# A float32 decoder layer in split products on one core: the point in the gated MLP from which products run side by side, moved by one unit

## The chip, the cores and the metric

The kernel runs on one core of a Trainium2 chip. The metric is the device time of one execution in microseconds (us). Three runs of the kernel before are given and their median is used; the profile is of one further execution, whose own time is shown beside its span.

## What is computed

The program is one decoder layer for 256 rows of 1024 channels: a norm, a combined projection, three attention mixers, gates, an output projection and a residual. Then comes the part that the change touches, a gated MLP with a causal convolution of width 3, and a last norm:

```python
def conv_ffn(x, w_up, conv_w, conv_b, w_down):
    h = x @ w_up
    h = lax.conv_general_dilated(h, conv_w[:, None, :].astype(h.dtype), window_strides=(1,),
                                 padding=[(CONV_WIDTH - 1, 0)],
                                 dimension_numbers=('NWC', 'WIO', 'NWC'),
                                 feature_group_count=h.shape[-1]) + conv_b
    a, u = jnp.split(h, 2, axis=-1)
    return (jax.nn.silu(a) * u) @ w_down
...
        x = x + conv_ffn(rmsnorm(x, norm_ffn[i]), w_up[i], conv_w[i], conv_b[i], w_down[i])
```

`w_up` is 1024 by 5632 (gate half and up half), `w_down` is 2816 by 1024.

## The kernel before

Every float32 operand of a large product is held as two fp32r parts, a high part (the value rounded) and a low part (the rest), and a product a·b is the sum of three: low·high, high·low and high·high. Weights arrive in tiles of 1 MB (class `Unit`, line 205): SyncE loads `raw` (line 217), ScalarE writes the high part `whi` in two halves (line 222), VectorE the low part `wlo` in two halves (line 226). There are five buffers for `raw` and five for each part, used in turn.

The MLP goes through 11 units (line 971, `i` from 0 to 10). A unit takes 256 channels of the gate half (tile `fa`), the same 256 of the up half (`fu`) and 256 rows of `w_down` (`fd`), and works on two chunks of 128 channels (line 977). A chunk has an up product with `fa` and one with `fu` (function `up`, line 980), a convolution of each on ScalarE and VectorE (lines 965 and 967, tile `cy`), silu and the gate product (lines 1001 and 1003, tile `sa`), the split of the result into `fh` and `fl` (lines 1006 and 1007) and, one chunk later, the 12 down products that add to four sums `acc` (line 1008, `later`, line 760).

An up product sums over 8 slices of 128 input channels (k) and gives 128 channels by 256 rows. It is written in two ways:

- In the units below `NORMED` (lines 983 to 986) it takes the activations without the factor of the norm. For each k, `mm3` (line 237) issues three matmuls of 256 columns, on lines 238, 239 and 240, with `h_hi` and `h_lo` (tile `hn`). The result is multiplied by the norm's factor row by row when VectorE takes it out of PSUM (`by_rstd`, line 864).
- From unit `NORMED` on (lines 987 to 998) it takes the normed activations from `h_parts` (tile `parts`), where high and low part lie beside each other. For each k one matmul of 512 columns (line 988) multiplies the high weights with both, and one of 256 columns (line 990) the low weights with the high activations. ScalarE copies one half of the PSUM bank (line 996), VectorE adds the other (line 997).

Unit 0 is computed before the loop (lines 883 to 951). `h_parts` is made by `norm_parts(i)` (line 874), called for two halves of the channels (line 976): VectorE multiplies `whole` (tile `gl`) by the norm's factor (line 876), ScalarE writes the high part (line 877), VectorE the low part (line 878), each on 128 by 1024 elements. It is called in unit `NORMED - 1`, after that unit's weight tiles have been asked for (lines 973 to 976).

An up product's result needs one of four PSUM banks (`bank`, line 742), which is free when line 864 (or 996 and 997) has read it. On an engine, instructions run in the order in which the scheduler has put them at compile time; in the MLP's loop that order is the scheduler's, not the program's, for VectorE, ScalarE and TensorE alike. An instruction that waits holds up all that stand behind it on its engine.

Of the kernel before, what the change touches and what calls it, by code (L numbers as in the profile page):

```python
# [15 lines left out]

P = 128
WARM = 9
NORMED = 3
S = 256  # L20
D = 1024
KC = D // P
# [107 lines left out]
def decoder_layer(ctx: ExitStack, tc, x, small_b, table, w1, wts, norms, out):  # L130
# [103 lines left out]
    def unit(name, steps=2, eng=None):  # L234
        return Unit(name).split(steps, eng)
# [506 lines left out]
    def bank():  # L742
        turn[0] ^= 1
        return pools[turn[0]].tile([P, 512], F32, name="g")
# [226 lines left out]
    for i in range(NFF // 2):  # L971
        with tc.issue_after(on_act[3 + i].ins) if i in (1, 2) else ExitStack():
            ua, uu, ud = [fu.pop(f"f{w}{i}", None) or unit(f"f{w}{i}") for w in "aud"]
        if i == NORMED - 1:
            for part in range(2):
                norm_parts(part)
        for c in range(2):
            ch = 2 * i + c

            def up(u):  # L980
                cols = slice(c * P, (c + 1) * P)
                ps = bank()
                if i < NORMED:
                    for k in range(KC):
# [102 lines left out]
```

## Time and profile before

| what | value |
|---|---|
| median of 3 runs | 424.89 us (424.8 to 426.27) |
| the profiled execution's own time | 424.76 us |
| its span | 423.0 us |
| TensorE, VectorE, ScalarE busy, share of the span | 98%, 74%, 61% |
| mean granted clock of TensorE | 0.996 |

The times are of whole executions; the profile covers the span from its first to its last instruction, 1.76 us less than that execution's time. A view by order of time gives the start and the duration of each instruction; consecutive instructions of an engine overlap a little, so what one adds to a full queue is the distance from its start to the start of the next, not its duration.

### The profile page before, as it was taken

Reading aid. Unit: us, or ns where it says so; the run is one execution under the profiler, and the core shown is the slowest. Engines: PE = TensorE matmul, PEld = TensorE weight load, DVE = VectorE, ACT = ScalarE, POOL = GpSimd, SP = SyncE. Lnnn points to the kernel's source line nnn. Section 1 sums busy time; section 2 is a strip of 40 time slices with the busy share of each in tenths; the row PEclk is TensorE's granted clock in tenths of the full one; section 3 lists DMA queues with packets and bytes.
Section 4 is the critical chain, followed back from the end, with each engine's and each line's share of the span. In section 5 each row is a group of like instructions: output and inputs, shape, how many; then the busy total and the mean of one; then the engine's idle time right before and its main releaser. Section 6 shows DMA issues by size and latency. Waiting matters only on the chain.

```text
span 423.0 us, 6337 instructions
## 1 busy us (share of the span) xinstructions
PE 412.4 (98%) x2407; PEld 347.8 (82%) x2407; DVE 313.2 (74%) x624; ACT 256.2 (61%) x451; POOL 18.3 (4%) x28
## 2 busy tenths in 40 slices
PE   8999999999999999999999999999999999999993
PEld 7998778776667888878788998988888888888883
DVE  3996653788784888434753899998797797887765
ACT  5843283547787855555434889467476576584633
POOL 2500010120000000000000000000000000000001
PEclk9999999999999999999999999999999999999998
DMA  8999419532227793645350465565652743800002
GB/s 279 416 375 407 146 34 354 198 131 100 101 100 248 292 381 109 229 184 198 107 192 0 149 253 198 200 251 200 245 212 105 283 187 110 299 0 2 0 2 99
DMA packets 12750, 78.00 MB, mean 184 GB/s; under 512 B 1408, under 2 KB 1424, under 8 KB 4912
## 3 DMA queue, kind: packets, MB, share of 16 engines
q1 hardware_dynamic: 12144, 75.48, 47.8%
q0 software_dynamic: 576, 2.12, 1.4%
q8 instruction: 19, 0.31, 0.3%
q14 instruction: 11, 0.09, 0.1%
HBM read 76.52 MB, written 1.07 MB: 183 GB/s over the span
## 4 chain that ended last, share of the span: by engine, by line
PE 82%; DVE 8%; ACT 5%; DMA 2%; issue 2%; SPq 0%; POOLq 0%; POOL 0%; ACTq 0%
PE g L988 12%; PE g L239 10%; PE g L240 10%; PE g L238 10%; PE g L990 6%; PE acc L238 6%; PE acc L240 6%; PE acc L239 6%; PE g L298 3%; DVE wlo L226 2%; PE g L888 2%; PE o L541 2%; DMA raw<-in_wts_dram 2%; PE g L426 2%; PE g L300 1%
## 5 line engine op out<-in xcount | busy, mean ns | idle before, releaser
L226 DVE TENSOR_TENSOR wlo<-raw,whi 128x1024 fp32r<-128x1024 f32 (+2 forms) x131 | 154.1, 1201 | 41.0 <-ACT whi L222 40.6
L222 ACT ACTIVATE whi<-raw 128x1024 fp32r<-128x1024 f32 (+2 forms) x130 | 130.2, 1040 | 50.5 <-PE g L240 34.3
L988 PE MATMUL g<-parts,whi 128*128 128x512 f32 x256 | 89.4, 396 | 0.0
L990 PE MATMUL g<-parts,wlo 128*128 128x256 f32 x256 | 66.2, 279 | 0.0
L988 PEld LDWEIGHTS g<-parts,whi 128*128 128x128 f32 x256 | 46.7, 188 | 9.2
L990 PEld LDWEIGHTS g<-parts,wlo 128*128 128x128 f32 x256 | 48.2, 188 | 2.8
L239 PE MATMUL g<-wlo,hn 128*128 128x512 f32 (+1 forms) x128 | 50.0, 391 | 0.0
L240 PE MATMUL g<-whi,hn 128*128 128x512 f32 (+1 forms) x128 | 50.0, 391 | 0.0
L238 PE MATMUL g<-whi,hn 128*128 128x512 f32 (+1 forms) x128 | 49.8, 390 | 0.0
L967 DVE SCALAR_TENSOR_TENSOR cy<-xn,small_b,cy 128x255 f32<-128x255 f32 (+1 forms) x88 | 41.5, 480 | 9.0 <-ACT cy L965 8.0
L238 PE MATMUL acc<-whi,fl 128*128 128x512 f32 (+1 forms) x88 | 34.2, 389 | 0.1
L239 PE MATMUL acc<-wlo,fh 128*128 128x512 f32 (+1 forms) x88 | 34.0, 386 | 0.0
L240 PE MATMUL acc<-whi,fh 128*128 128x512 f32 (+1 forms) x88 | 34.0, 386 | 0.0
L965 ACT ACTIVATE cy<-xn,small_b 128x256 f32<-128x256 f32 x44 | 25.8, 598 | 7.4 <-DVE xn L997 7.4
L239 PEld LDWEIGHTS g<-wlo,hn 128*128 128x128 f32 x128 | 24.1, 188 | 5.1 <-issue 0.9
L240 PEld LDWEIGHTS g<-whi,hn 128*128 128x128 f32 x128 | 24.1, 188 | 4.2 <-issue 0.2
L238 PEld LDWEIGHTS g<-whi,hn 128*128 128x128 f32 x128 | 24.1, 189 | 4.0 <-ACT whi L222 0.2
L426 PE MATMUL g<-hn,whi 128*128 128x512 f32 x72 | 26.2, 405 | 0.0
L996 ACT ACTIVATE xn<-g 128x256 f32<-128x256 f32 x32 | 12.2, 380 | 22.2 <-PE g L988 22.2
L428 PE MATMUL g<-hn,wlo 128*128 128x256 f32 x72 | 19.9, 292 | 0.0
L997 DVE TENSOR_TENSOR xn<-g,xn 128x256 f32<-128x256 f32 x32 | 13.5, 421 | 8.3 <-ACT xn L996 8.3
L240 PEld LDWEIGHTS acc<-whi,fh 128*128 128x128 f32 x88 | 16.5, 188 | 3.4
(213 smaller groups left out, 698.6 us busy)
## 6 DMA issues: line engine op xcount, KB each, us to landing
raw<-in_wts_dram SPq DMA_DIRECT2D x61, 1024.0 KB, 4.8
gl<-in_w_dram SPq DMA_DIRECT2D x8, 512.0 KB, 7.6
raw<-in_wts_dram SPq DMA_DIRECT2D x5, 512.0 KB, 7.4
raw<-in_wts_dram SPq DMA_DIRECT2D x2, 804.0 KB, 9.0
T<-tvd POOLq DMA_DIRECT2D x1, 1280.0 KB, 16.3
xs<-in_x_dram SPq DMA_DIRECT2D x2, 516.0 KB, 3.8
out_dram<-raw SPq DMA_DIRECT2D x4, 256.0 KB, 2.1
T<-tvd POOLq DMA_DIRECT2D x1, 768.0 KB, 9.6
```

The costliest lines, as they stand in the source:

```text
L222: nc.scalar.activation(self.parts[0][:, sl], self.raw[:, sl], AF.Copy)
L226: return (eng or nc.vector).tensor_sub(self.parts[1][:, sl], self.raw[:, sl], self.parts[0][:, sl].bitcast(F32))
L238: nc.tensor.matmul(ps, al, bh, start=start, stop=False)
L239: nc.tensor.matmul(ps, ah, bl, start=False, stop=False)
L240: nc.tensor.matmul(ps, ah, bh, start=False, stop=stop)
L426: hi = lambda: nc.tensor.matmul(ps, view(0, k), h_parts[:, k].rearrange("p a q -> p (a q)"), start=k == 0, stop=k == KC - 1)
L428: lo = lambda: nc.tensor.matmul(ps[:, :S], view(1, k), h_hi[:, k, :], start=False, stop=False)
L965: on_act.append(nc.scalar.activation(y, u, AF.Identity, bias=vec_c[:, 3, ch:ch + 1], scale=vec_c[:, 2, ch:ch + 1]))
L967: nc.vector.scalar_tensor_tensor(y[:, sh:], u[:, :S - sh], vec_c[:, w, ch:ch + 1], y[:, sh:], op0=ALU.mult, op1=ALU.add)
L988: hi = lambda: nc.tensor.matmul(ps, u[0][:, k, cols], h_parts[:, k].rearrange("p a q -> p (a q)"), start=k == 0, stop=k == KC - 1)
L990: lo = lambda: nc.tensor.matmul(ps[:, :S], u[1][:, k, cols], h_parts[:, k, 0, :], start=False, stop=False)
L997: nc.vector.tensor_add(v, ps[:, :S], part)
```

## The change

One constant is smaller by one:

```diff
-NORMED = 3
+NORMED = 2
```

So `norm_parts` is called in unit 1, after unit 1's weight tiles and before its products (line 974), and unit 2 takes the second form of the up product (line 983). The four up products of unit 2 are then 32 matmuls of 512 columns and 32 of 256 in place of 96 of 256, and their results leave PSUM through lines 996 and 997 in place of line 864. The scheduler orders the loop anew.

On VectorE, the place is in unit 1 and the start of unit 2. In the names, `sa_2531` and `fl_2539` belong to chunk 0, `fl_2555` to chunk 1, `wlo_2572` to `fd` of unit 1, `g_2578` to `g_2689` (before) and `g_2584` to `g_2695` (after) are unit 1's four up products, and `wlo_2738` (before) and `wlo_2744` (after) are the low part of unit 2's `fa`. Before, from chunk 1's convolution to the first half of unit 2's `fa`:

```order
L967 SCALAR_TENSOR_TENSOR cy_2549<-xn1_2267,small_b_389,cy_2549 128x255
L226 TENSOR_TENSOR wlo_2572<-raw_2570,whi_2571 128x1024
L967 SCALAR_TENSOR_TENSOR cy_2549<-xn1_2267,small_b_389,cy_2549 128x254
L226 TENSOR_TENSOR wlo_2572<-raw_2570,whi_2571 128x1024
L1003 TENSOR_TENSOR sa_2546<-sa_2546,cy_2549 128x256
L967 SCALAR_TENSOR_TENSOR cy_2604<-xn1_2267,small_b_389,cy_2604 128x255
L967 SCALAR_TENSOR_TENSOR cy_2636<-xn1_2267,small_b_389,cy_2636 128x255
L1007 TENSOR_TENSOR fl_2555<-sa_2546,fh_2554 128x256
L967 SCALAR_TENSOR_TENSOR cy_2604<-xn1_2267,small_b_389,cy_2604 128x254
L967 SCALAR_TENSOR_TENSOR cy_2636<-xn1_2267,small_b_389,cy_2636 128x254
L864 TENSOR_TENSOR xn1_2267<-g_2657,xn1_2267 128x256
L226 TENSOR_TENSOR wlo_2738<-raw_2736,whi_2737 128x1024
```

And now, first the stretch that begins with the two multiplications of line 876:

```order
L876 TENSOR_TENSOR gl_2269<-gl_2269,xn1_2267 128x1024
L1003 TENSOR_TENSOR sa_2531<-sa_2531,cy_2533 128x256
L967 SCALAR_TENSOR_TENSOR cy_2549<-xn1_2267,small_b_389,cy_2549 128x255
L876 TENSOR_TENSOR gl_2270<-gl_2270,xn1_2267 128x1024
L1007 TENSOR_TENSOR fl_2539<-sa_2531,fh_2538 128x256
L967 SCALAR_TENSOR_TENSOR cy_2549<-xn1_2267,small_b_389,cy_2549 128x254
L226 TENSOR_TENSOR wlo_2572<-raw_2570,whi_2571 128x1024
L1003 TENSOR_TENSOR sa_2546<-sa_2546,cy_2549 128x256
L226 TENSOR_TENSOR wlo_2572<-raw_2570,whi_2571 128x1024
L1007 TENSOR_TENSOR fl_2555<-sa_2546,fh_2554 128x256
L878 TENSOR_TENSOR parts_2268<-gl_2269,parts_2268 128x4x256
L878 TENSOR_TENSOR parts_2268<-gl_2270,parts_2268 128x4x256
```

and the rows that follow it directly, down to the first half of unit 2's `fa`:

```order
L864 TENSOR_TENSOR xn1_2267<-g_2584,xn1_2267 128x256
L864 TENSOR_TENSOR xn1_2267<-g_2616,xn1_2267 128x256
L864 TENSOR_TENSOR xn1_2267<-g_2663,xn1_2267 128x256
L967 SCALAR_TENSOR_TENSOR cy_2610<-xn1_2267,small_b_389,cy_2610 128x255
L967 SCALAR_TENSOR_TENSOR cy_2642<-xn1_2267,small_b_389,cy_2642 128x255
L967 SCALAR_TENSOR_TENSOR cy_2610<-xn1_2267,small_b_389,cy_2610 128x254
L967 SCALAR_TENSOR_TENSOR cy_2642<-xn1_2267,small_b_389,cy_2642 128x254
L967 SCALAR_TENSOR_TENSOR cy_2689<-xn1_2267,small_b_389,cy_2689 128x255
L864 TENSOR_TENSOR xn1_2267<-g_2695,xn1_2267 128x256
L1003 TENSOR_TENSOR sa_2614<-sa_2614,cy_2642 128x256
L967 SCALAR_TENSOR_TENSOR cy_2689<-xn1_2267,small_b_389,cy_2689 128x254
L226 TENSOR_TENSOR wlo_2744<-raw_2742,whi_2743 128x1024
```

Before, one row of line 876 stood ahead of the first half of unit 2's `fa`, and both rows of line 878 and the other of line 876 far behind it; now all four stand ahead of it, and three rows of line 864, which free PSUM banks and feed ScalarE's convolutions, have come behind them.

On TensorE, the place is where unit 2's up products begin (`g_2766` in both programs, and after also `g_2831`, the product of the same weights for the second chunk; `whi_2737` and `wlo_2738` before, `whi_2743` and `wlo_2744` after are the two parts of unit 2's `fa`, `fl_2642` and `fl_2648` chunk 2's result). Before, after the last row of unit 1's fourth up product `g_2689`:

```order
L240 MATMUL g_2689<-hn_2265,whi_2462 128x256
L238 MATMUL g_2766<-hn_2265,wlo_2738 128x256
L239 MATMUL g_2766<-hn_2265,whi_2737 128x256
L240 MATMUL g_2766<-hn_2265,whi_2737 128x256
L238 MATMUL g_2766<-hn_2265,wlo_2738 128x256
L238 MATMUL acc00_2523<-whi_2571,fl_2642 128x512
```

and now, after the last two rows of that product (`g_2695`):

```order
L239 MATMUL g_2695<-hn_2265,whi_2462 128x256
L240 MATMUL g_2695<-hn_2265,whi_2462 128x256
L988 MATMUL g_2766<-parts_2268,whi_2743 128x512
L988 MATMUL g_2831<-parts_2268,whi_2743 128x512
L990 MATMUL g_2766<-parts_2268,wlo_2744 128x256 x2
L988 MATMUL g_2766<-parts_2268,whi_2743 128x512
L238 MATMUL acc00_2523<-whi_2571,fl_2648 128x512
```

In both, the low part of unit 2's `fa` is first read at the boundary between unit 1's and unit 2's up products, and the down products of chunk 2 stand behind. Now the two matmuls ahead of it read the normed activations and the high part. On SyncE and GpSimd the rows are the same as before.

## Rows read from the trace of the kernel before

**Rows 1.** The page, engines' busy time, and the chain that ended last, by engine
```profile
PE 412.4 (98%) x2407; PEld 347.8 (82%) x2407; DVE 313.2 (74%) x624; ACT 256.2 (61%) x451; POOL 18.3 (4%) x28
...
PE 82%; DVE 8%; ACT 5%; DMA 2%; issue 2%; SPq 0%; POOLq 0%; POOL 0%; ACTq 0%
```

**Rows 2.** Waits of TensorE over the whole span (us in total, times, longest): the first
```profile
PE g L325 <- DVE whi L308: 1.3, 2, 0.9
```

**Rows 3.** Busy time by stretch: PE, PEld, DVE, ACT, POOL, then clock, DMA, GB/s
```profile
251.65:277.34 25.69, 25.69 (x172) 23.70 (x171) 25.59 (x41) 20.03 (x29) 0.00 (x0) 1.00 0.48 170
...
300.00:400.00 100.00, 100.00 (x535) 85.87 (x535) 80.91 (x135) 64.22 (x110) 0.00 (x0) 1.00 0.38 141
```

**Rows 4.** Order of time on TensorE (start us, us, what)
```profile
243.25 0.28 PE L238 MATMUL g<-hn,wlo 128*128 128x256 f32 x1
...
251.65 0.47 PE L238 MATMUL acc<-whi,fl 128*128 128x512 f32 x1
251.95 0.40 PE L239 MATMUL acc<-wlo,fh 128*128 128x512 f32 x1
...
256.28 0.40 PE L238 MATMUL acc<-whi,fl 128*128 128x512 f32 x1
...
259.03 0.28 PE L239 MATMUL g<-hn,whi 128*128 128x256 f32 x1
...
260.34 0.28 PE L238 MATMUL g<-hn,wlo 128*128 128x256 f32 x1
...
280.90 0.40 PE L988 MATMUL g<-parts,whi 128*128 128x512 f32 x1
...
283.72 0.40 PE L988 MATMUL g<-parts,whi 128*128 128x512 f32 x1
```

**Rows 5.** Order of time on VectorE (start us, us, what)
```profile
248.88 0.42 DVE L864 TENSOR_TENSOR xn<-g,xn 128x256 f32<-128x256 f32 x1
...
249.61 0.42 DVE L864 TENSOR_TENSOR xn<-g,xn 128x256 f32<-128x256 f32 x1
249.95 1.22 DVE L876 TENSOR_TENSOR gl<-gl,xn 128x1024 f32<-128x1024 f32 x1
251.08 0.42 DVE L1007 TENSOR_TENSOR fl<-sa,fh 128x256 fp32r<-128x256 f32 x1
251.41 0.48 DVE L967 SCALAR_TENSOR_TENSOR cy<-xn,small_b,cy 128x255 f32<-128x255 f32 x1
251.81 1.22 DVE L226 TENSOR_TENSOR wlo<-raw,whi 128x1024 fp32r<-128x1024 f32 x1
252.94 0.48 DVE L967 SCALAR_TENSOR_TENSOR cy<-xn,small_b,cy 128x254 f32<-128x254 f32 x1
...
257.06 1.21 DVE L226 TENSOR_TENSOR wlo<-raw,whi 128x1024 fp32r<-128x1024 f32 x1
...
267.31 1.22 DVE L878 TENSOR_TENSOR parts<-gl,parts 128x1024 fp32r<-128x1024 f32 x1
```

**Rows 6.** Order of time on ScalarE (start us, us, what)
```profile
255.34 1.99 ACT L222 ACTIVATE whi<-raw 128x1024 fp32r<-128x1024 f32 x2
257.24 0.40 ACT L1001 ACTIVATE sa<-cy 128x256 f32<-128x256 f32 x1
257.55 0.59 ACT L965 ACTIVATE cy<-xn,small_b 128x256 f32<-128x256 f32 x1
258.04 1.04 ACT L877 ACTIVATE parts<-gl 128x1024 fp32r<-128x1024 f32 x1
```

**Rows 7.** The page, groups by line: busy us, mean ns, idle before
```profile
L988 PEld LDWEIGHTS g<-parts,whi 128*128 128x128 f32 x256 | 46.7, 188 | 9.2
...
L996 ACT ACTIVATE xn<-g 128x256 f32<-128x256 f32 x32 | 12.2, 380 | 22.2 <-PE g L988 22.2
```

**Rows 8.** Busy time by stretch as in rows 3, at the end of the program
```profile
416.00:418.00 2.00, 0.53 (x5) 0.32 (x3) 1.50 (x5) 1.55 (x6) 0.15 (x1) 1.00 0.35 131
418.00:423.00 5.00, 0.00 (x0) 0.00 (x0) 0.75 (x1) 0.72 (x1) 0.40 (x1) 0.64 0.42 157
```

## The prediction

> **What bounds the kernel now.** I read the page first: TensorE is busy for 98% of the span and carries 82% of the chain that ended last; VectorE, with 74%, is second [rows 1]. The view of TensorE's waits lists five pairs, the longest in total 1.3 us, and all five belong to the parts ahead of the MLP [rows 2]. By stretches, TensorE has no gap from 251.65 to 277.34 us nor from 300 to 400 us, at a granted clock of 1.00 (2.4 GHz) [rows 3]. So in the MLP the time is the sum of what TensorE issues, and a change can gain only by taking work from TensorE and lose only by making it wait; what it loses isn't paid back, since there is no later gap to swallow it. The second thing to see in [rows 3] is that VectorE is busy for 25.59 of the 25.69 us in the very stretch into which the change moves VectorE's work, but for 81 of the later 100 us.
>
> **What TensorE saves.** The views by order of time give the distances from start to start. Between 243.25 and 251.65 stand 70 matmuls of 256 columns (counted in the program's order), 0.120 us each, so a k in the old form costs 0.360 us. Twelve down products take 259.03 - 256.28 = 2.75 us, 0.229 us per matmul of 512 columns. Eight k in the new form take 283.72 - 280.90 = 2.82 us, 0.3525 us for each [rows 4]. Unit 2 has 4 up products of 8 k: 32 x 0.0075 = **0.24 us saved**. It is small because both forms stream 768 columns for a k; only one matmul in three goes away.
>
> A rule of the Trainium skill promises more. The row: a weight load lasts 188 ns [rows 7], but a load and its matmul of 256 columns together advance TensorE by 0.120 us [rows 4], so the loads lie under the matmuls. The rule ("TensorE: Matmul & The Clock Gate", The mechanism, in the part on packing small matmuls): a weight load overlaps with running matmuls only where the two use different row groups of the array, so here it would not; and a load of 128 columns takes 107 ns (LDWEIGHTS, same page). By it 32 fewer loads would save an estimated 3.4 us, and the sum would be 0.8 us faster after the wait found below. The trace disagrees: 0.120 us leaves no room for that beside 256 columns.
>
> **What moves on VectorE.** The number of rows stays: line 997 replaces line 864 four times, at the same size. ScalarE gets four more copies of line 996, 0.38 us each [rows 7], 1.5 us on an engine that is idle for 5.7 us of [rows 3]'s first stretch; I cost them at nothing, and if that cover is gone they lengthen the wait for ScalarE, not TensorE's work. SyncE's and GpSimd's rows are the same; the weights' buffers are released some us later where the low parts are made later, and the trace has no wait of the MLP for a landing, so I take nothing there either.
>
> What costs is the order. Up to 248.88 VectorE's rows are the same. From there, 23 rows stand ahead of the first low half of unit 2's `fa` in the changed program (the second and third VectorE excerpts). Six of them work on 128 by 1024 elements (two each of lines 876, 226 and 878): 252.94 - 251.81 = 1.13 us each, and 251.08 - 249.95 = 1.13 for line 876; line 878, of the same size, as these. Eight are of line 967: 251.81 - 251.41 = 0.40. Nine are small (three of line 1003, two of 1007, four of 864): 249.95 - 249.61 = 0.34 and 251.41 - 251.08 = 0.33 [rows 5]. Sum: 6 x 1.13 + 8 x 0.40 + 9 x 0.335 = 6.78 + 3.20 + 3.02 = 13.0 us. So the low half begins at 261.88 and, with 1.21 us for itself, ends at 263.09.
>
> To this come two short gaps. The convolutions of unit 1 can start on ScalarE only when line 864 has read its bank, 0.42 us [rows 5], and last 0.59 us, 0.49 from one to the next [rows 6]. VectorE reaches its first line 967 about 1.0 us after the first of the three rows of line 864, when the first convolution's 0.42 + 0.59 is just over, and the second one 0.40 later, when the second's +0.49 is just over: 0.1 us in all. **The low half is ready at about 263.2 us**; before, it began at 257.06 [rows 5].
>
> **When TensorE wants it.** Before, TensorE reached its first matmul with that low half at 260.34 [rows 4], 2 us after it was ready, so the slack was there. The changed program has the same work up to that point (unit 1's four up products, the down products of chunks 0 and 1), then two matmuls of 512 columns: 260.34 + 2 x 0.23 = 260.80. The high half that these two read must come from ScalarE: behind three convolutions whose first starts when line 864 lets it. By VectorE's sum line 864 begins at 257.80 (248.88 + 8.92: the first twelve rows), so the three run from 258.3 to 259.8 at 0.49 each, and the high half takes 1.04 us, to 260.8. That delays the two matmuls by some 0.5 us, inside the wait that follows.
>
> How long TensorE takes from a release to full pace is shown once: `fl` of chunk 0 ended at 251.08 + 0.42 = 251.50 [rows 5]; the down products' second matmul started at 251.95, where 251.65 + 0.23 was due [rows 4], so pace was resumed as from 251.72, 0.22 us after the release. So the first matmul with the low half starts at 263.2 + 0.2 = 263.4 instead of 260.8: **a wait of 2.6 us**. The down products of chunk 2 behind it need the very next row of VectorE, 0.34 us later, and TensorE is then busy with the four matmuls ahead of them for 0.6 us: no further wait. The other low halves come every 1 to 2 us from there, while unit 2's up products take 2.8 us each: I count no second wait.
>
> **Sum.** + 2.6 - 0.24 = + 2.4 us. Against the profiled execution: span 423.0 + 2.4 = 425.4, time 424.76 + 2.4 = 427.2; against the median of the runs, which lies 0.13 us higher, 424.89 + 2.4 = **427.3 us**, 0.56% slower. Its bounds: without gaps and without the 0.22 us the wait is 263.09 - 260.80 = 2.3 us, 426.9; with gaps of 0.5 us on VectorE and the saving not realised it is 3.0 us, 427.9.
>
> **Rivals.**
> - *The cover holds.* TensorE reaches the low half after it is ready, as before, where the slack was 2 us; it decides at the first matmul of line 990, if VectorE finishes that half before 260.8. Then only the saving is left: 424.89 - 0.24 = 424.65, not slower. For it: no MLP wait exists now [rows 2]. Against it: VectorE would have to do 13.0 us of rows in 10.5, and has no gap to close in that stretch [rows 3]. Chance 0.10.
> - *The clock falls in the wait.* After its last matmul the granted clock stays 1.00 in the stretch to 418 us, in which TensorE is busy for 0.53 of 2 us, and is 0.64 on average in the 5 us without any matmul [rows 8]. At 1.2 GHz all of those 5 us would read 0.50, so 0.72 of them, 3.6 us, were at the lower level. If the 2.6 us wait brought as long a stretch at half pace, it would cost 1.8 us more: 429.1. Against it: the stretch with 1.5 us of idleness didn't lower it. Chance 0.05.
> - *A second wait.* Unit 2's `fu` or `fd` low halves, which stand behind the same queue, are late by one row of 1.13 us: 428.4. Chance 0.03.
> - *Loads count.* Each of the 32 loads taken away gives back its 188 ns: 6.0 us, 427.3 + 0.24 - 6.0 = 421.5. [rows 4] speaks against it. Beside it stands the skill's rule above. Chance 0.02.
> - That the change doesn't do what it says is excluded by the order: the new form stands there for unit 2.
>
> **Numbers.** The forecast has the remaining chance, 0.80. A measurement of this kernel can tell about 0.5%, 2.1 us, from no change, so "slower" begins at 427.0. The forecast's bounds, 426.9 to 427.9, lie mostly above: I put 0.61 of its 0.80 there and 0.19 below. Slower: 0.61 + 0.05 + 0.03, taken as 0.68; within 0.5%: 0.19 + 0.10, taken as 0.30; faster: 0.02. The range takes in the forecast's bounds, widened by 0.5 to 0.7 us because the runs shown differ by 1.5 us and the durations are rounded, and the second wait: 426.2 to 428.4; it leaves out the cover that holds, the clock and the loads, 0.17.
>
> **What would show it.** Right: TensorE's waits list line 990 (or its load) behind line 226 with some 2.6 us, near 261 to 263.4 us, preceded by some 0.5 us of line 988 behind ScalarE's line 222; VectorE is without a gap from 249 to 263; the new form appears 32 k times more, at 0.3525 us; the last 100 us look as before, moved by 2.4 us. Wrong: no gap in TensorE there (then the cover held and the sum of VectorE's rows was too high), a granted clock under 1.00 after the gap, a wait of unit 2's later products, or k in the new form that take less than 0.35 us.

## The result, and the profile after

| what | before | after |
|---|---|---|
| median of the compared runs | 424.85 us (6 runs, 424.58 to 426.27) | 428.42 us (6 runs, 427.22 to 428.66) |
| the profiled execution's own time | 424.76 us | 427.22 us |
| its span | 423.0 us | 425.2 us |

The ratio is 1.0071, with a 95% interval of 1.0053 to 1.009: slower by 0.7% (the quotient of the two medians is 1.0084). Forecast were 427.3 us and a range of 426.2 to 428.4, so the sign was right; the median lies at the range's upper end, 0.02 us above it, and 1.1 us over the forecast. The profiled execution (427.22) is the lowest of the six. It shows the forecast's mechanism almost to the tenth of a microsecond; what lies between it and the other five is a second effect, which took the experiments to find.

The page of after, engines' busy time, the chain by engine, and the groups of lines 988 and 990, which answer to [rows 1, 7]:

```profile
PE 412.2 (97%) x2375; PEld 345.4 (81%) x2375; DVE 313.8 (74%) x624; ACT 257.1 (60%) x455; POOL 18.3 (4%) x28
...
PE 77%; DVE 12%; ACT 5%; issue 2%; DMA 2%; SPq 0%; POOLq 0%; POOL 0%; ACTq 0%; DVEq 0%
...
L988 PE MATMUL g<-parts,whi 128*128 128x512 f32 x288 | 100.8, 396 | 0.4 <-ACT whi L222 0.4
L990 PE MATMUL g<-parts,wlo 128*128 128x256 f32 x288 | 74.5, 279 | 1.7 <-DVE wlo L226 1.7
```

TensorE has 32 matmuls fewer, and two idle times that did not exist: 0.4 us ahead of line 988 and 1.7 us ahead of line 990. VectorE's share of the chain went from 8% to 12%. Where it happens, in order of time on TensorE (start us, us, what, and in brackets the idle time before it and its releaser):

```profile
260.85 0.73 PE L988 MATMUL g<-parts,whi 128*128 128x512 f32 x2 [0.36 <-ACT whi L222]
263.31 0.50 PE L990 MATMUL g<-parts,wlo 128*128 128x256 f32 x2 [1.73 <-DVE wlo L226]
263.65 0.40 PE L988 MATMUL g<-parts,whi 128*128 128x512 f32 x1
263.88 0.39 PE L238 MATMUL acc<-whi,fl 128*128 128x512 f32 x1
...
266.61 0.28 PE L990 MATMUL g<-parts,wlo 128*128 128x256 f32 x1
...
267.67 0.28 PE L990 MATMUL g<-parts,wlo 128*128 128x256 f32 x1
```

Before, the first matmul with the low half started at 260.34 [rows 4]; now at 263.31, behind two of line 988 that take 0.46. That is 2.5 us later than the same queue without a wait (260.80). The two matmuls of line 990 behind the release take 0.34 us instead of 0.24 (263.31 to 263.65), so what follows is 2.6 us late. Down products follow at 263.88 without a gap. What TensorE waited for, in order of time on VectorE:

```profile
248.80 1.22 DVE L876 TENSOR_TENSOR gl<-gl,xn 128x1024 f32<-128x1024 f32 x1
...
250.67 1.22 DVE L876 TENSOR_TENSOR gl<-gl,xn 128x1024 f32<-128x1024 f32 x1
...
255.47 2.36 DVE L878 TENSOR_TENSOR parts<-gl,parts 128x1024 fp32r<-128x1024 f32 x2
257.75 1.08 DVE L864 TENSOR_TENSOR xn<-g,xn 128x256 f32<-128x256 f32 x3
258.90 2.16 DVE L967 SCALAR_TENSOR_TENSOR cy<-xn,small_b,cy 128x255 f32<-128x255 f32 x5
260.97 0.42 DVE L864 TENSOR_TENSOR xn<-g,xn 128x256 f32<-128x256 f32 x1
261.31 0.42 DVE L1003 TENSOR_TENSOR sa<-sa,cy 128x256 f32<-128x256 f32 x1
261.64 0.48 DVE L967 SCALAR_TENSOR_TENSOR cy<-xn,small_b,cy 128x254 f32<-128x254 f32 x1
262.03 1.22 DVE L226 TENSOR_TENSOR wlo<-raw,whi 128x1024 fp32r<-128x1024 f32 x1
```

and on ScalarE, the high half that line 988 waited for:

```profile
258.26 1.59 ACT L965 ACTIVATE cy<-xn,small_b 128x256 f32<-128x256 f32 x3 [3.72 <-DVE xn L864]
259.76 1.04 ACT L222 ACTIVATE whi<-raw 128x1024 fp32r<-128x1024 f32 x1
```

By stretch (columns as in [rows 3]), the loss is in one place, and the rest is full as before:

```profile
260.50:263.80 3.30, 1.22 (x5) 0.79 (x6) 3.30 (x8) 3.30 (x7) 0.00 (x0) 1.00 0.00 0
263.80:277.00 13.20, 13.20 (x70) 11.23 (x69) 12.96 (x19) 9.52 (x14) 0.00 (x0) 1.00 0.73 263
300.00:400.00 100.00, 100.00 (x534) 85.79 (x533) 81.18 (x135) 63.14 (x108) 0.00 (x0) 1.00 0.39 144
```

### The profile page after: what moved, and what is told of

It reads as the page before. It is cut to its first block, busy times and chain, and to the rows that moved or that the text cites. A ratio compares the mean times of both kernels' runs of the same rounds, so it can differ in the third digit from the quotient of the medians.

```text
span 425.2 us, 6279 instructions
## 1 busy us (share of the span) xinstructions
PE 412.2 (97%) x2375; PEld 345.4 (81%) x2375; DVE 313.8 (74%) x624; ACT 257.1 (60%) x455; POOL 18.3 (4%) x28
## 4 chain that ended last, share of the span: by engine, by line
PE 77%; DVE 12%; ACT 5%; issue 2%; DMA 2%; SPq 0%; POOLq 0%; POOL 0%; ACTq 0%; DVEq 0%
PE g L988 13%; PE g L239 8%; PE g L240 8%; PE g L238 8%; PE g L990 7%; PE acc L238 5%; PE acc L239 5%; PE acc L240 5%; DVE wlo L226 4%; PE g L298 3%; DVE cy L967 2%; PE g L888 2%; PE o L541 2%; DMA raw<-in_wts_dram 2%; PE g L426 2%
## 5 line engine op out<-in xcount | busy, mean ns | idle before, releaser
L988 PE MATMUL g<-parts,whi 128*128 128x512 f32 x288 | 100.8, 396 | 0.4 <-ACT whi L222 0.4
L990 PE MATMUL g<-parts,wlo 128*128 128x256 f32 x288 | 74.5, 279 | 1.7 <-DVE wlo L226 1.7
L988 PEld LDWEIGHTS g<-parts,whi 128*128 128x128 f32 x288 | 52.5, 188 | 10.9 <-ACT whi L222 0.6
L990 PEld LDWEIGHTS g<-parts,wlo 128*128 128x128 f32 x288 | 54.2, 188 | 5.2 <-DVE wlo L226 2.2
L996 ACT ACTIVATE xn<-g 128x256 f32<-128x256 f32 x36 | 13.6, 378 | 22.3 <-PE g L988 22.2
L997 DVE TENSOR_TENSOR xn<-g,xn 128x256 f32<-128x256 f32 x36 | 15.2, 422 | 9.5 <-ACT xn L996 9.5
```

The lines of the kernel that those rows point to most:

```text
L988: hi = lambda: nc.tensor.matmul(ps, u[0][:, k, cols], h_parts[:, k].rearrange("p a q -> p (a q)"), start=k == 0, stop=k == KC - 1)
L990: lo = lambda: nc.tensor.matmul(ps[:, :S], u[1][:, k, cols], h_parts[:, k, 0, :], start=False, stop=False)
L997: nc.vector.tensor_add(v, ps[:, :S], part)
```

## The experiments

The first four ask whether the order on VectorE is the cause, and whether it is all of it.

**The changed kernel once more.** No edit.

> The changed kernel once more, for the part of its time that its profile does not hold: that execution took 427.2 us, the other five 428.1 to 428.7 at a mean granted clock of 0.992 to 0.994 instead of 0.996. Theory A (queue: TensorE waits 2.6 us for the first low half of unit 2's fa, which now stands behind 13 us of VectorE's rows) and with it theory C (in most executions the granted clock falls in that wait, and about 1.2 us more are lost behind it): most executions at 428.1 to 428.7, and a profile of such an execution shows a granted clock below 1.00 in the stretches just behind 263 us and some 1.2 us more there. Rival D (the 1.2 us are noise of the chip, or lie elsewhere): the times spread evenly from 427 to 429, or a slow profile shows its loss at the start or the end.

Measured: 427.82 us median of 6 runs (426.99 to 428.95), ratio 1.0057 (1.0037 to 1.0078). There are two levels: three runs at 427.0 to 427.2 with a mean granted clock of 0.996 to 0.998, three at 428.4 to 429.0 with 0.993. The profiled execution is one of the second kind: span 426.8. Its waits in the MLP are those of the first profile (1.7 us at line 990, 0.3 at line 988) at a clock of 1.00. The difference lies at the start of the program. In order of time on TensorE, then by stretch (the clock is the third number from the end):

```profile
9.28 0.39 PE L325 MATMUL g<-parts,whi 128*128 128x256 f32 x1 [1.88 <-DVE whi L308]
...
11.00:12.00 1.00, 1.00 (x6) 1.00 (x7) 1.00 (x4) 1.00 (x3) 1.00 (x2) 0.64 1.05 438
12.00:13.00 1.00, 1.00 (x7) 1.00 (x7) 1.00 (x5) 1.00 (x2) 1.00 (x2) 0.50 1.00 426
13.00:14.00 1.00, 1.00 (x6) 1.00 (x6) 1.00 (x4) 1.00 (x3) 0.78 (x2) 0.50 0.96 395
14.00:15.00 1.00, 1.00 (x8) 1.00 (x7) 1.00 (x3) 1.00 (x4) 0.16 (x1) 0.65 1.03 415
```

and the same wait in the first profile of after:

```profile
9.13 0.39 PE L325 MATMUL g<-parts,whi 128*128 128x256 f32 x1 [1.29 <-DVE whi L308]
```

In the repeated execution TensorE waits 1.88 us for line 308, where the first profile of after has 1.29 and that of before 0.86; then the clock is at its lower level (1.2 of 2.4 GHz) for a while, where the other two profiles have 1.00. The four stretches lose 4 x 1 - (0.64 + 0.50 + 0.50 + 0.65) = 1.7 us, the difference of the spans is 426.8 - 425.2 = 1.6. This stands 250 us ahead of the change. Theory C expected the low clock behind 263 us; in this execution it is at the start.

**The parts early, unit 2 in its old form.**

```diff
-                if i < NORMED:
+                if i < NORMED + 1:
```

> One part of the change alone: the parts are made one unit sooner, unit 2 keeps the three matmuls of 256 columns. Theory A: the first low half is ready at 263.2 us as in the changed kernel, but its first reader stands two matmuls of 512 columns earlier, at 260.3, so the wait is 2.9 to 3.2 us; without the saving of 0.24 us the time is 424.85 + 3.1 = 428.0 us, and with the clock's loss in most executions about 429.2. Rival B (the second form is what costs, by its copies on ScalarE or its two matmuls that need the high half): the time is that of before, 424.9, within 0.5 us.

Measured: 428.68 us median of 4 runs (427.91 to 432.24), ratio 1.0092 (1.0056 to 1.0128). The two runs at a mean granted clock of 0.996 took 427.9 and 428.0, as forecast without a fall of the clock; the others took 429.32 (0.993) and 432.24 (0.985), and no profile shows what the last one lost. The profiled execution has a span of 426.0, 3.0 us over before's, with a clock of 1.00 from 8 to 412 us. Its wait in the MLP:

```profile
PE g L238 <- DVE wlo L226: 2.8, 1, 2.8
```

The loss is there without a matmul of unit 2 in the new form, at the same row of VectorE. The order costs, not the form. It costs 0.8 us more span than with the new form: 0.24 is the saving that is missing, and 0.46 are the two matmuls of line 988 that in the change fill a part of the wait.

**The low parts on GpSimd.**

```diff
-        nc.vector.tensor_sub(h_parts[:, sl, 1, :], whole[i], h_parts[:, sl, 0, :].bitcast(F32))
+        nc.gpsimd.tensor_sub(h_parts[:, sl, 1, :], whole[i], h_parts[:, sl, 0, :].bitcast(F32))
```

> The changed kernel with line 878 (the low half of the normed activations) on GpSimd instead of VectorE: two rows of 1.13 us leave VectorE's queue, and in the order that results three more rows (lines 864, 1003, 967, together 1.07 us) fall behind unit 2's fa. Theory A: the low half is ready at 263.2 - 3.3 = 259.9 us, before TensorE wants it at 260.6: no wait over 0.3 us, and only the saving of 0.24 us is left, 424.6 us, at a clock of 0.996. Two GpSimd rows of about 2.7 us (twice the 1.36 us of its 512 columns) end near 258.6, in time. Rival B: the second form's cost stays, 427 us or more. A third outcome, that GpSimd's rows slow VectorE's, would show as VectorE rows longer than 1.22 us and a rest of the wait.

Measured: 427.57 us median of 6 runs (427.38 to 427.97), ratio 1.005 (1.0033 to 1.0068): no gain, though two rows of 1.13 us have left VectorE. Theory A's 424.6 failed. The wait at line 990 is 2.3 us, and none of the six runs has the low clock (0.995 to 0.997). In order of time on VectorE, then on GpSimd:

```profile
255.98 1.08 DVE L864 TENSOR_TENSOR xn<-g,xn 128x256 f32<-128x256 f32 x3
257.13 5.21 DVE L967 SCALAR_TENSOR_TENSOR cy<-xn,small_b,cy 128x255 f32<-128x255 f32 x5
262.27 1.21 DVE L226 TENSOR_TENSOR wlo<-raw,whi 128x1024 fp32r<-128x1024 f32 x1
...
253.70 7.18 POOL L878 TENSOR_TENSOR parts<-gl,parts 128x1024 fp32r<-128x1024 f32 x2 [19.87 <-ACT parts L877]
```

Five rows of line 967 take 5.21 us where after has 2.16. Shown singly, the first two last 1.49 and 2.62 us instead of 0.48, and GpSimd's two rows 4.63 and 2.59. The second row of line 967 comes to an end 0.3 us after GpSimd's second row does (258.54 + 2.62 = 261.16, 253.70 + 7.18 = 260.88). So 3.05 us were given back in waiting for 2.26 us of rows taken away. The Trainium skill has the rule for it ("SBUF — State Buffer", SBUF: two separate sides): a GpSimd instruction that reads SBUF and a VectorE operation with two SBUF inputs need one shared pair of ports, the first holds it for its whole instruction, and the other stands still. The rows agree: line 864, which reads one of its inputs from PSUM, keeps its pace beside GpSimd (1.08 us for three). The order theory is neither supported nor hurt by this run: the low half ended at 263.48, and TensorE waited for it.

**The low parts twice.** Line 878 is issued two times, with the same values.

```diff
         nc.vector.tensor_sub(h_parts[:, sl, 1, :], whole[i], h_parts[:, sl, 0, :].bitcast(F32))
+        nc.vector.tensor_sub(h_parts[:, sl, 1, :], whole[i], h_parts[:, sl, 0, :].bitcast(F32))
```

> The changed kernel with line 878 issued twice (the same values written again): two more rows of 1.13 us ahead of unit 2's fa on VectorE. Theory A: the wait grows by 2.26 us, from 2.6 to 4.9 us in all; without a lower clock 427.3 + 2.3 = 429.6 us, with the clock's loss of 1.2 us or more (theory C) 430.8 us or more, and then in every execution, since the wait is longer. Rival B: VectorE's extra rows cost nothing, 428.4 as the changed kernel.

Measured: 432.03 us median of 4 runs (430.78 to 432.16), ratio 1.0148 (1.0126 to 1.017); span 430.2, 5.0 us over the profile of after. The waits in the MLP, and the stretches behind them (lines 988 and 990 have the numbers 989 and 991 here):

```profile
PE g L989 <- ACT whi L222: 2.6, 1, 2.6
PE g L991 <- DVE wlo L226: 1.7, 1, 1.7
...
264.00:266.00 2.00, 0.27 (x2) 0.22 (x2) 2.00 (x5) 2.00 (x5) 0.00 (x0) 0.60 0.00 0
266.00:268.00 2.00, 2.00 (x6) 1.70 (x7) 2.00 (x5) 2.00 (x3) 0.00 (x0) 0.50 0.00 0
268.00:270.00 2.00, 2.00 (x6) 1.53 (x5) 2.00 (x3) 2.00 (x3) 0.00 (x0) 0.50 0.61 139
270.00:272.00 2.00, 2.00 (x8) 1.59 (x8) 2.00 (x4) 1.61 (x3) 0.00 (x0) 0.69 1.09 418
```

Two rows more on VectorE make the low half 2.5 us later (it ends at 264.50 + 1.22 = 265.72, against 263.25), which is the order's price as before. The other half is the clock: it fell in the longer waits, and matmuls of 512 columns then stand 0.427 us apart. At the start, from 9 to 18 us, the clock of this execution was 1.00. All four runs have a mean clock of 0.992 or less, as theory C expected of the longer wait. So the rival of the clock was not dead, and the question became whether it also strikes behind the change's own, shorter wait.

**The wait taken away.** `norm_parts` is called between unit 1's two chunks.

```diff
-        if i == NORMED - 1:
-            for part in range(2):
-                norm_parts(part)
         for c in range(2):
             ch = 2 * i + c
+            if i == NORMED - 1 and c == 1:
+                for part in range(2):
+                    norm_parts(part)
```

> The changed kernel with norm_parts called between unit 1's two chunks instead of ahead of the first. The work is the same, instruction for instruction; in VectorE's order one row of line 878 and one of line 876 come behind more of unit 1's rows, the other row of line 878 behind the first low half of unit 2's fa, and the three rows of line 864 ahead of them. Theory A (the loss is the order on VectorE: four rows of 1.13 us ahead of that low half): the waits at lines 988 and 990 go, and only the saving of 0.24 us is left against the kernel before: 424.85 - 0.24 = 424.6; span of an execution with an undisturbed start 422.8. Rival F (VectorE is too full between 249 and 277 us for 4.5 us more, wherever they stand): the wait moves to a later low half of unit 2 and 1 to 2 us of loss stay: 426 to 427. Rival C (the second form costs more than the first once it runs without a wait): 425.5 or more without a wait.

Measured: 424.91 us median of 12 runs (424.55 to 426.33), ratio 0.9992 (0.9976 to 1.0007). The waits of TensorE list none between 238 and 405 us. In order of time on VectorE, one row of line 878 now stands behind the low half and the other well ahead, with line 864 between:

```profile
258.31 1.22 DVE L878 TENSOR_TENSOR parts<-gl,parts 128x1024 fp32r<-128x1024 f32 x1
...
261.25 0.42 DVE L864 TENSOR_TENSOR xn<-g,xn 128x256 f32<-128x256 f32 x1
261.58 1.22 DVE L226 TENSOR_TENSOR wlo<-raw,whi 128x1024 fp32r<-128x1024 f32 x1
262.82 1.23 DVE L878 TENSOR_TENSOR parts<-gl,parts 128x1024 fp32r<-128x1024 f32 x1
```

Same work, another order, and the loss is gone. The new form and the four ScalarE copies cost nothing that can be measured; the saving of 0.24 us fits the medians, but is too small to be shown by them. (This execution began late, with a wait of 2.0 us at line 325 and a clock of 0.50 from 12 to 14 us behind it.) But two orders have moved: TensorE now does chunk 2's twelve down products, 261.90 to 264.64, ahead of unit 2, so it came 2.75 us later to the half. Without that, it would have begun unit 2 at 261.90, wanted the half one matmul of line 988 later, at 262.13, and found it at 261.58 + 1.22 = 262.80: some 0.7 us late. How far VectorE's order alone carries, the last experiment below tells.

**The start filled.** Six matmuls on zeros where TensorE waits for line 308, in the changed kernel (three times), in the kernel before, and in the version above.

```diff
         nc.tensor.matmul(pt[:16, :384], tb[:, R_RB:R_RB + 16], tb[:, R_OH:R_OH + 384], start=True, stop=True)
+        for _ in range(6):
+            nc.tensor.matmul(a0_ps[0][:, :P], idle, idle, start=True, stop=True)
```

> The changed kernel with one addition at the start of the program: behind line 332, six more of the matmuls of line 288 (128 columns, on zeros, 0.15 us from start to start) into a PSUM bank that the first product of line 325 then begins anew. They stand where TensorE otherwise waits for line 308. Two executions of the changed kernel have been profiled: one took 427.22 us with a wait of 1.29 us there and a granted clock of 1.00 behind it; the repetition took 428.58 us, with a wait of 1.88 us and a granted clock of 0.64, 0.50, 0.50 and 0.65 in the four microseconds from 11 us on. Theory (what lies between 427.2 and 428.4 is lost at the start, where the clock falls behind a longer wait, and has nothing to do with the change): the wait shrinks to some 0.5 to 1.0 us, the clock stays at 1.00 there, and all runs stand at 427.0 to 427.5; none above 428. Rival (the second level is made by the change, in the MLP): runs at 428.1 to 428.9 stay as frequent as in the changed kernel (eight of twelve). The wait of 1.7 us at line 990 behind line 226 stays under both.

> Both edits together: norm_parts between unit 1's two chunks, and the six matmuls behind line 332. If both theories hold, all runs stand at 424.4 to 424.9 and none near 426; the median is 0.1 to 0.4 us under the kernel before's, less than a measurement can tell, and the highest run 1.5 us under the kernel before's highest. If only the order counts, some runs still stand near 426.

> The kernel before, with the six matmuls behind line 332 and nothing else. Its own runs have two levels too, 424.6 to 425.3 and 426.0 to 426.5. Theory (start): only the lower level is left, median 424.8, highest under 425.4; if the six matmuls reach past the arrival of what line 325 waits for (the profiled execution of the kernel before waited 0.86 us there, the six take 0.9), up to 0.2 us more. Rival (the levels come from elsewhere): runs at 426.0 to 426.5 in about a third.

> The changed kernel with the six matmuls at the start, as before. That start took the low clock out of 22 of 22 runs of two kernels without the wait at line 990 (mean granted clock 0.994 to 0.998), but two of the four runs of this one stood at 428.7 us with 0.992 and 0.993. Theory G (in a part of the executions the granted clock falls in the MLP too, behind the wait at line 990): about half of the runs at 0.992 to 0.993 and 1.6 to 1.8 us over the others, which stand at 427.0; where the profiled execution is one of them, the granted clock is under 1.00 in the 4 us behind line 990 and 1.00 from 8 to 240 us. Rival (the start still falls in some executions): the low clock lies between 8 and 16 us. Rival (chance in the four runs): none of twelve at 0.993 or under.

> The same kernel once more, since a profile shows one execution and the question is where the clock falls in one of the longer ones: theory G, behind the wait at line 990 near 262 to 266 us; rival, between 8 and 16 us; rival, nowhere, and the longer ones wait somewhere else. Chances for this execution to be a longer one: about one half.

| kernel | runs | median, us (range) | ratio (interval) | mean clock 0.993 or under |
|---|---|---|---|---|
| before, all runs with a clock on record | 67 | 424.99, 425.04, 425.7, 424.82 by comparison | | 21 |
| parts between the chunks | 12 | 424.91 (424.55 to 426.33) | 0.9992 (0.9976 to 1.0007) | 4 |
| the same, start filled | 12 | 425.01 (424.47 to 426.04) | 0.9983 (0.997 to 0.9996) | 0 |
| before, start filled | 10 | 424.76 (424.37 to 427.14) | 0.999 (0.9974 to 1.0006) | 0 |
| weights ahead of the parts, start filled (below) | 12 | 425.33 (424.94 to 426.17) | 1.0006 (0.9993 to 1.0018) | 0 |
| after, both times | 12 | 428.42 and 427.82 | 1.0071 and 1.0057 | 7 |
| after, start filled, three times | 4, 6, 6 | 428.73, 428.17, 427.58 | 1.0079, 1.0057, 1.0051 | 7 |

With the start filled, no run of the three kernels without the long wait at line 990 has the low clock, 0 of 34. With the start as it was, two of these kernels were run, and 25 of their 79 runs have it. So the second level of these two comes from the start. But the changed kernel keeps its second level: 7 of 16 runs, at 428.4 to 429.1 us, while eight others stand at 427.0 to 427.9 (one, 430.04 at 0.997, lost its time in a way that no profile shows). The expectation that all would stand at 427.0 to 427.5 failed. Of the three profiles, two (427.01 and 427.48 us) have the same waits in the MLP at a clock of 1.00. The third, of the second time, is one of the longer executions (429.06 us, span 427.3) and shows where the clock falls now. In order of time on TensorE, then by stretch (in this kernel the lines 988 and 990 have the numbers 990 and 992):

```profile
263.84 0.50 PE L992 MATMUL g<-parts,wlo 128*128 128x256 f32 x2 [1.72 <-DVE wlo L226]
...
264.65 0.59 PE L239 MATMUL acc<-wlo,fh 128*128 128x512 f32 x1
265.04 0.63 PE L240 MATMUL acc<-whi,fh 128*128 128x512 f32 x1
265.46 0.63 PE L238 MATMUL acc<-whi,fl 128*128 128x512 f32 x1
...
264.00:266.00 2.00, 2.00 (x8) 1.61 (x9) 2.00 (x5) 2.00 (x3) 0.00 (x0) 0.67 0.00 0
266.00:268.00 2.00, 2.00 (x6) 1.54 (x5) 2.00 (x4) 2.00 (x3) 0.00 (x0) 0.50 0.61 143
268.00:270.00 2.00, 2.00 (x12) 1.71 (x11) 2.00 (x3) 1.68 (x3) 0.00 (x0) 0.98 1.11 410
```

The same wait (0.38 and 1.72 us), and 0.8 us behind it matmuls of 512 columns come to stand 0.42 us apart. The loss is 2 x (0.33 + 0.50 + 0.02) = 1.7 us, and 427.3 less the 425.6 of the third time's profile, which has no such fall, is 1.7. From 8 to 240 us the clock was 1.00. So the clock can fall in the MLP too. One profile shows it; that the other six runs with the low clock lost theirs there as well is inferred from their times and from the filled start.

The version with both edits is the only one that lies under the kernel before with its whole interval, by 0.17% (0.04 to 0.3%), about 0.7 us; its highest run is 426.04, where before has 426.76. This is no gain of the moved parts: the medians are equal (425.01 and 425.04), 8 of the 28 runs of before that it is compared with have the low clock, and the other 20 have a median of 424.95. The start-filled kernels still have a few higher runs at a clock of 0.996; the profile of one (427.14 us, the kernel before with its start filled) shows waits of 1.0 us at line 238 for line 729 and 0.7 for line 804, which are lines 727 and 802 without the edit. The profile of before doesn't list them, and they have nothing to do with the change.

**VectorE's order alone.** The changed kernel, start filled, with one line that asks for unit 2's `fa` before `norm_parts`.

```diff
         if i == NORMED - 1:
+            fu[f"fa{i + 1}"] = unit(f"fa{i + 1}")
             for part in range(2):
                 norm_parts(part)
```

> The changed kernel with the start filled, and with one line more: unit 2's fa tile is asked for ahead of norm_parts in unit 1. TensorE's order up to unit 2's first matmul is that of the changed kernel (the version with norm_parts between the chunks had also put chunk 2's twelve down products ahead of it, 2.75 us, so there TensorE came later as well as VectorE sooner). On VectorE both halves of that tile's low part now stand ahead of the two rows of line 878, and fu's stand behind them. Order theory: the wait of 1.7 us at fa's first low half goes, since that half ends some 5 us sooner. Line 878's rows come 2.3 us later and end near 260.1, TensorE wants the parts at 260.8: no wait for them, 0.4 at most. fu's first low half then ends near 266.5 (260.0 plus three rows of 0.335, five of 0.40, one of 1.13, two of 0.34, and its own 1.2, with short gaps for ScalarE's convolutions), where TensorE wants it at about 266.1: a wait of some 0.5 us. Sum 424.85 + 0.5 + 0.4 - 0.24 = 425.5, 424.7 to 425.8 for most runs. Clock theory: with waits this short no run has the low clock (mean 0.994 or more). Rival (VectorE's fill alone decides, not what stands ahead): 2 us or more of waits in the MLP, 427 us.

Measured: 425.33 us median of 12 runs (424.94 to 426.17), ratio 1.0006 (0.9993 to 1.0018), none with the low clock. In order of time on VectorE (line numbers are 2 to 3 higher here: 880 is line 878), then on TensorE (991 and 993 are lines 988 and 990):

```profile
253.63 2.35 DVE L226 TENSOR_TENSOR wlo<-raw,whi 128x1024 fp32r<-128x1024 f32 x2
...
256.24 1.22 DVE L226 TENSOR_TENSOR wlo<-raw,whi 128x1024 fp32r<-128x1024 f32 x1
257.37 2.36 DVE L880 TENSOR_TENSOR parts<-gl,parts 128x1024 fp32r<-128x1024 f32 x2
...
259.85 0.28 PE L240 MATMUL g<-hn,whi 128*128 128x256 f32 x1
260.12 0.50 PE L991 MATMUL g<-parts,whi 128*128 128x512 f32 x1
260.46 0.40 PE L993 MATMUL g<-parts,wlo 128*128 128x256 f32 x2
...
266.61 0.50 PE L993 MATMUL g<-parts,wlo 128*128 128x256 f32 x2
```

TensorE comes to unit 2 at 259.85 + 0.12 = 259.97 (260.33 in the profile of after; this execution had been 0.36 us ahead since the start of the MLP), with unit 1 done and chunk 2's down products still behind. Ahead of that its work is the same, only chunk 1's down products stand ten matmuls later. The second of the two rows in the first line is the first low half of `fa`, the next line the second: both now stand ahead of the parts, and TensorE loses 0.15 us at unit 2's start and 0.1 at `fu`'s first low half (266.61, where 266.03 + 2 x 0.23 = 266.49 was due) instead of 2.5. So it is the order on VectorE that makes the wait at line 990 and takes it away; ScalarE's high halves of `fa` come sooner in this order too, so the 0.4 us at line 988 aren't told apart from it. The loss is not all gone: the median stands 0.5 us above before's, and 0.6 above that of before's runs without the low clock (424.70, 12 of the 17 compared). The profile shows about half of it.

## Why the prediction was right, and where it was not

- **The walk along VectorE** was right: the low half was to begin at 261.88, with the two gaps at about 262.0, and be ready at 263.2; it began at 262.03 and ended at 263.25. So were the 1.13, 0.40 and 0.335 us taken for its rows.
- **ScalarE's high half**, forecast for 260.8, ended at 259.76 + 1.04 = 260.80; the wait for it is 0.36 us (about 0.5 forecast).
- **The wait**, 2.6 us by start, is 263.31 - 260.80 = 2.5, and 2.6 for what stands behind it. The view shows TensorE idle for 3.30 - 1.22 = 2.1 us of it; the rest is the end of the last matmul ahead of each of the two gaps, which the view still counts as busy. (Behind the wait stand three matmuls ahead of the down products, not four; they took 0.57 us, and no wait followed, as forecast.)
- **The saving**: three k in unit 2 take 267.67 - 266.61 = 1.06 us, 0.353 for each, as taken. 2.6 - 0.24 = 2.4 against 2.2 of measured span; the 0.2 us between them stay unexplained. The time grew by 2.46, because the part of it outside the span was 2.02 us in this execution and 1.76 in that of before. That 427.22 meets the forecast's 427.2 so closely is luck; the span, 425.2 against 425.4, shows how well the sum fits.
- **No second wait, no load that counts**: both rivals fell. TensorE's 13.20 us behind the wait are full, and 32 loads less gave nothing that is seen.
- **The rival of the clock was judged wrongly.** The sentence "the stretch with 1.5 us of idleness didn't lower it" took one execution's behaviour in one place for that of all. The clock falls behind this wait in some executions and not in others, so the case had to be split over executions, and 0.05 was far too little: 7 of 16 runs with the start filled have the low clock. Its price was well sized: 1.8 forecast, 1.7 measured. The forecast's 427.3 holds for executions without a fall (427.0 to 427.2 at the first two comparisons), and 428.1 to 429.0 is that plus one fall, in the MLP or at the start. The range left the fall out and reached up to 428.4 for a second wait that didn't come; that the median lies at its end is luck, since a fall, not a second wait, put it there.
- **A step that was missing**: the three runs shown of before, 424.80, 424.89 and 426.27, lie at these two levels too (no clock is on record for them). I counted their difference as width, and did not ask which mechanism made it. The place to look was behind line 325's 1.3 us in [rows 2], though that profile itself has a clock of 1.00 there.

Open: why the clock falls behind the same wait in one execution and not in the next; whether a fall at the start and one in the MLP exclude each other; why the six runs with the parts on GpSimd (wait 2.3 us) and the profiled execution with the parts early (2.8 us) had none; and what 432.24 and 430.04 us were made of.

## What to carry to other kernels

Work that moves earlier onto an engine without a gap is not free because the engine is "only" 74% busy: walk its order row by row to the first row that TensorE needs, and compare the two times. If it comes late, try another place for the moved work before giving up the change: half a unit later the same rows cost nothing measurable here, behind one weight tile some 0.5 us. And a wait of TensorE has two prices, its length and a possible fall of the clock behind it; the second differs between executions, so look at the spread of the runs and their granted clocks before calling a level the kernel's time.

## What the hardware showed that was not expected

- The granted clock fell behind waits of 1.88 us (start) and of 0.38 and 1.72 us with two matmuls between (MLP), to 0.50, and cost 1.6 to 1.7 us each; behind waits of 1.29 us (start) and 0.36 and 1.73 us (MLP) in other executions it stayed at 1.00. The length of the wait alone doesn't decide it: the clock also stayed at 1.00 behind one wait of 2.8 us (parts early) and one of 2.3 (parts on GpSimd) in the MLP, and behind one of 1.8 us at the start (low parts twice).
- The wait at the start gets longer when the work ahead of it is done sooner: the last two matmuls ahead of it (line 332) began at 7.54, 7.03 and 6.58 us (before, after, after again), the first one behind it at 9.22, 9.13 and 9.28. With matmuls on zeros in that wait none of the 34 runs of three kernels has the low clock.
- A subtraction of 128 by 1024 elements on GpSimd lasted 2.59 us (4.63 where it seems to have waited itself), against 1.13 on VectorE, and VectorE's rows of line 967 stood still beside it, 2.62 us instead of 0.48.
